# Keys of two heads from one product, and a state-space scan in two strides, in one fused transformer layer

## The chip, the cores and the metric

One Trainium2 chip, one core. The kernel is one launch that computes a whole layer. The metric is the device time of a run in microseconds (us); the kernel before takes 1132.93 us (median of three runs).

## The reference, cut to what matters

The layer mixes tokens in two parallel groups (attention and a state-space layer), projects them back, and then runs a mixture of 32 experts. 1024 latent tokens and 256 context tokens, width 1024, 8 heads.

```python
def mla_project(...):            # per head: 64 key columns without rotation, 32 shared rotary ones
    kv = (rms_norm(ckv, kv_norm_g) @ w_ukv).reshape(*lead, N_HEADS, QK_NOPE_DIM + V_HEAD_DIM)
    k_nope, v = kv[..., :QK_NOPE_DIM], kv[..., QK_NOPE_DIM:]
...
def mla_attend(q_nope, q_rope, k_nope, k_rope, v):
    s = einsum('bqhd,bkhd->bhqk', q_nope, k_nope) + einsum('bqhr,bkr->bhqk', q_rope, k_rope)
    return einsum('bhqk,bkhd->bqhd', softmax(s * SOFTMAX_SCALE), v)
...
def s5_states(u, s0, abar, bbar, reverse):   # x[n] = abar * x[n-1] + (bbar u)[n], complex, per direction
    bu = einsum('bngh,gph->bngp', u, bbar);  bu[:, 0] += abar * s0
    return associative_scan(combine, (abar, bu), axis=1)
```

The context tokens are scanned first from a zero state; the latent scan starts from the context's last state.

## The kernel before, in words

**Order.** All engines run instruction lists written out by hand; the order of the calls in the code is the order on each engine, and loads issued on SP's queue start in that order too. Waits between engines follow from which instruction last wrote or read the same addresses.

**Memory.** `Mem` (line 50) hands out one large SBUF arena in slots of 1024 f32 for each partition (some fifty). `alloc` (line 59) takes a wanted slot (`at`) or else, for sizes of whole slots, the aligned place whose contents were freed longest ago in the order of the code (`c[np.argmin(w[c])]`); a place that was freed most recently comes last. `free` only notes the order. Whoever writes a place next waits on the chip until its last reader is done.

**The scan.** Tokens are grouped in chunks of 8, so that there are 32 context and 128 latent chunks. `chunk_input(g)` (line 796) computes, for each of 32 groups, what a chunk adds to the state, into `Wc` (32 chunks) and `Wl` (128 chunks), with 2 x 32 f32 for each chunk and partition (real and imaginary parts, 32 groups; both directions and 64 states lie on the partitions). Lines 1194 to 1199 then run the recurrence over chunks on GpSimd (POOL), one chunk after the other: a product of the last state with `a8` (the eighth power of abar as a 2 x 2 form, 128 elements for each partition) into `sw`, and two additions of 64 elements. `xc` keeps the state after the context.

```python
    for n in range(1, 160):
        tt(sw.f, Wn(n - 1)[:, None].to_broadcast([128, 2, 2, G]), a8.f, OP.mult, Gp)
        tt(Wn(n), Wn(n), sw.f[:, 0], OP.add, Gp)
        tt(Wn(n), Wn(n), sw.f[:, 1, ::-1], OP.add, Gp)
```

**Attention.** The loop at line 1200 runs over heads h = -1 to 7, and for each over ten key tiles kt of 128 keys. In h = -1 it computes the `values` of each tile, the row maxima (`peak`) of head 0, and one step of `ada()` for each kt; in the other rounds `scores` of the head, `gain` (weights times values), the maxima of the next head and the queries of the head after it. Products in f32 precision are three matmuls of rounded halves (`mm3`, lines 258 to 260). `keys(nxt)` and `keys_c(nxt)` at kt = 0 of round h compute head h+1's 64 key rows for the latent and the context keys and split them into a rounded part `kh` (ScalarE, ACT) and a rest `kl` (VectorE, DVE). Three pairs of PSUM banks go round (`ring2`).

**ada.** `ada()` (line 1012) multiplies the modulation vectors with 16 blocks of 1 MB (`in_wada`), loaded on SP (line 1018) into a buffer of two slots each, one step for each kt of h = -1 and of h = 0, to kt = 6; the block loaded in step n is used by the matmuls of line 1022 in step n+1. In the kernel before the first four blocks lie from slots 12, 20, 24 and 26, and the next ones in the same four places in turn, to the end of h = -1.

**Before the loop.** Lines 1174 to 1190 compute head 0's keys and queries among the last chunk inputs. `shared(i)` (line 845) copies the rotary key rows from `kr` (slots 6.88 to 8.12), the second time just ahead of the scan, and then `kr` and `U` (slots 24 to 29, the chunk inputs' moving operand) are freed.

**Who reads the scan.** `readout()` (line 1031) is stepped from round h = 6 on: at kt = 1 its first loads, at kt = 3 `state(0)`, which copies `Wl` on DVE (line 1053) and ACT.

Of the kernel before, what the change touches and what calls it, by code (L numbers as in the profile page):

```python
# [16 lines left out]
OP = mybir.AluOpType  # L17
# [4 lines left out]
NT = 1024  # L22
NC = 256
H = 8
NOPE, ROPE, VD = 64, 32, 64
G, P, HG = 32, 64, 16
# [197 lines left out]
def body(ctx, tc, a, out):  # L224
    nc = tc.nc
    V, A, Gp, PE, SP = nc.vector, nc.scalar, nc.gpsimd, nc.tensor, nc.sync
# [7 lines left out]
    ps = pp.tile([128, 8, 512], F32, name="ps")  # L234

    def buf(*shape, name="", at=None, zone=None):
        return Buf(nc, zone or mem, shape, name, at)
# [9 lines left out]
    def cp(o, i, scale=1.0):  # L247
        A.activation(o, i, AF.Copy, scale=scale)  # L248

    def tt(o, x, y, op, e=None):  # L250
        (e or V).tensor_tensor(o, x, y, op=op)  # L251

    def split(lo_r, raw, hi_r, hi_f):
        cp(hi_r, raw)
        tt(lo_r, raw, hi_f, OP.subtract)

    def mm3(o, lh, ll, rh, rl, start, stop_):
        PE.matmul(o, lh, rh, start=start, stop=False)  # L258
        PE.matmul(o, lh, rl, start=False, stop=False)  # L259
        PE.matmul(o, ll, rh, start=False, stop=stop_)  # L260
# [25 lines left out]
    a8 = buf(2, 2, G, name="a8", at=-1)  # L286
# [7 lines left out]
    sw, xc = buf(2, 2, G, name="scan", at=-1), buf(2, G, name="xc", at=-1)  # L294
# [447 lines left out]
    for i in range(3):  # L742
# [3 lines left out]
        for ft in (2, 3):  # L746
            b = rA()
# [31 lines left out]
    Wl = buf(128, 2, G, name="Wl", at=-1)  # L779
    Wc = buf(32, 2, G, name="Wc", at=-1)  # L780
# [12 lines left out]
    def Wn(n):  # L793
        return Wc.f[:, n] if n < 32 else Wl.f[:, n - 32]

    def chunk_input(g):
        wi, gl, b = wis[g // 8], g % 8, rS()
        for ri in range(2):
            o = slice(ri * 160, ri * 160 + 160)
            PE.matmul(ps[0:64, b, o], wi.f[:, gl, ri, 0:64], U.f[:, g, 0:160], start=True, stop=True)  # L800
            PE.matmul(ps[64:128, b, o], wi.f[:, gl, ri, 64:128], U.f[:, g, 32:192][:, ::-1],
                      start=True, stop=True)
        src = ps[:, b, 0:320].rearrange("p (r n) -> p r n", r=2)
        for w_, c0, n in ((Wc, 0, 32), (Wl, 32, 128)):
            dst = w_.f[:, :, :, g].rearrange("p n r -> p r n")
            if g % 2:
                cp(dst, src[:, :, c0:c0 + n])
            else:
                V.tensor_copy(dst, src[:, :, c0:c0 + n])  # L809
        if gl == 7:  # L810
            wi.free()

    rS = Ring([6, 7])
    wkv_l, wkv_h = buf(D, name="wkv_l", at=10), buf(D, name="wkv_h", at=10)
# [18 lines left out]
    ring2 = Ring([(0, 1), (2, 3), (4, 5)])  # L833
    NB = 2
    kh = [buf(NT + NC, name="kh", at=33) for _ in range(NB)]
    kl = [buf(NT + NC, name="kl", at=33) for _ in range(NB)]
    rS.items = [6, 7, 3]
    for g in range(16, 24):
        chunk_input(g)
        side_.tick()  # L840
        if g > 21:
            k = g - 22
            split(wuq_l[k].r, wuq_l[k].f, wuq_h[k].r, wuq_h[k].g)

    def shared(i):

        V.tensor_scalar(kh[i].r[96:97, :], kr.f[64:65], 0.0, 1.0, op0=OP.mult, op1=OP.add)
        cp(kh[i].r[64:96], kr.f[64:96])
        tt(kl[i].r[64:96], kr.f[64:96], kh[i].g[64:96], OP.subtract)
# [5 lines left out]
    def flat(d):  # L855
        return ps[:, d[0]:d[0] + 2, :].rearrange("p a n -> p (a n)")

    def ck(o, n):
        lo, hi = ckn[o // 512]
        return hi.r[:, o % 512:o % 512 + n], lo.r[:, o % 512:o % 512 + n]  # L860
# [6 lines left out]
    def values(kt):  # L867
        mm3(ps[:, 6, :], *ck(kt * 128, 128), wkv_h.r[:, 512:], wkv_l.r[:, 512:], True, True)
        cp(v.f[:, kt], ps[:, 6, :])

    def keys(a_):
        d, i = ring2(), a_.i
        for hf in range(2):
            mm3(ps[0:64, d[hf], :], wkv_h.r[:, a_.hs], wkv_l.r[:, a_.hs], *ck(hf * 512, 512), True, True)
        p = flat(d)[0:64]
        cp(kh[i].r[0:64, 0:NT], p)
        tt(kl[i].r[0:64, 0:NT], p, kh[i].g[0:64, 0:NT], OP.subtract)

    def keys_c(a_):
        b, i = ring2()[0], a_.i  # L880
        p = ps[0:64, b, 0:NC]
        mm3(p, wkv_h.r[:, a_.hs], wkv_l.r[:, a_.hs], *ck(NT, NC), True, True)
        cp(kh[i].r[0:64, NT:], p)
        tt(kl[i].r[0:64, NT:], p, kh[i].g[0:64, NT:], OP.subtract)

    def queries(a_):
        d = a_.d = ring2()
# [23 lines left out]
    def peak(a_, q):  # L911

        if q == 0:
            a_.mx = buf(2, 8, name="mx")
        d = ring2()
        for hf in range(2):
            PE.matmul(ps[:, d[hf], :], a_.qh.r[0:96, q * 128:(q + 1) * 128],  # L917
                      kh[a_.i].r[0:96, hf * 512:hf * 512 + 512], start=True, stop=True)
        V.reduce_max(a_.mx.f[:, 0, q:q + 1], flat(d), axis=AX.X)  # L919
# [22 lines left out]
    def scores(a_, kt):  # L942
        i, xh, x = a_.i, a_.qh, a_.ql
        ks = slice(kt * 128, (kt + 1) * 128)
        d = ring2()
        for hf in range(2):
            o, q_ = ps[:, d[hf], :], slice(hf * 512, hf * 512 + 512)
            PE.matmul(o, kh[i].r[0:97, ks], xh.r[0:97, q_], start=True, stop=False)  # L948
            PE.matmul(o, kh[i].r[0:96, ks], x.r[0:96, q_], start=False, stop=False)
            PE.matmul(o, kl[i].r[0:96, ks], xh.r[0:96, q_], start=False, stop=True)  # L950
        p = a_.p[kt] = buf(NT, name="P")
        A.activation(p.f, flat(d), AF.Exp, scale=SCALE)  # L952

    def gain(a_, kt):

        p = a_.p[kt]
        for hf in range(2):
            PE.matmul(ps[hf * 64:hf * 64 + 64, 6, :], v.f[:, kt, a_.hs], p.f[:, hf * 512:hf * 512 + 512],  # L958
                      start=kt == 0, stop=kt == NK - 1)
        if kt == 1:  # L960
            a_.acc = buf(NT, name="acc")
            tt(a_.acc.f, a_.p[0].f, p.f, OP.add)
            a_.p[0].free()
        elif kt:
            tt(a_.acc.f, a_.acc.f, p.f, OP.add)
        if kt:
            p.free()
        if kt == NK - 1:
            a_.o = buf(512, name="o")
            cp(a_.o.f, ps[:, 6, :])  # L970
            a_.ql.free(), a_.qh.free()
# [200 lines left out]
    TILES = ((), (0,), (1,), (2, 3), (4,), (5,), (6,), (7,), (), ())  # L1172
    heads = [Head(h) for h in range(H)]
    side_.drain()
    shared(0)
    keys(heads[0])
    keys_c(heads[0])
    chunk_input(24)
    chunk_input(25)
    queries(heads[0])  # L1180
# [10 lines left out]
    for w_ in (ccl, sig, shx, scx):  # L1191
        w_.free()
    v = buf(NK, 512, name="v", at=28)
    for n in range(1, 160):
        tt(sw.f, Wn(n - 1)[:, None].to_broadcast([128, 2, 2, G]), a8.f, OP.mult, Gp)
        tt(Wn(n), Wn(n), sw.f[:, 0], OP.add, Gp)
        tt(Wn(n), Wn(n), sw.f[:, 1, ::-1], OP.add, Gp)
        if n == 31:
            Gp.tensor_copy(xc.f, Wn(31))
    for h in range(-1, H):  # L1200
        cur, nxt, nn, prev = (heads[i] if 0 <= i < H else None for i in (h, h + 1, h + 2, h - 1))
        for kt in range(NK):
            if cur and nxt and kt == 0:
                keys(nxt)
                keys_c(nxt)
            if cur:
                scores(cur, kt)
            else:
                values(kt)
                next(aux, None)  # L1210
            if kt:
                if cur:
                    gain(cur, kt - 1)
            elif prev:
                gain(prev, NK - 1)
            if prev and 1 <= kt <= 4:
                (sums, inverse, divide, finish_head)[kt - 1](prev)
            if nxt:
                for q in TILES[kt]:
                    peak(nxt, q)  # L1220
                if kt in (1, 5):
                    peak_c(nxt, kt - 1)
                if kt == 7:
                    peak_all(nxt)
                if kt == 8:
                    peak_row(nxt)
            if nn:
                if kt == 7:
                    queries(nn)
                    turned(nn)  # L1230
                if kt == 8:
                    rotate(nn)
                if kt == 9:
                    parts(nn)
            if h == 0:
                next(aux, None)
            if h == 0 and kt == 5:
                Wc.free()
            if h == H - 2 and kt == 1:
                for w_ in [wkv_l, wkv_h] + wuq_l + wuq_h + [w_ for q in ckn + cqn[0] + cqn[1] for w_ in q]:  # L1240
                    w_.free()
                cs.free(), bada.free()
            if (h - H + 2) * NK + kt == RO or (h - H + 2) * NK + kt >= RO2:
                next(ro, None)
            if (h, kt) == (H - 2, 3) or h == H - 1 and kt:
                next(sd, None)
# [139 lines left out]
    for ft in range(4):  # L1386
        d = rG_()
# [609 lines left out]
    o = ps[:, 7, 0:256].rearrange("p (a n) -> p a n", a=2)  # L1997
# [6 lines left out]
    for s in range(8):  # L2004
        mm(s, 0)
        i = s - 1
# [177 lines left out]
```

## Time and profile before

| | |
|---|---|
| median of three runs | 1132.93 us (1132.74 to 1136.99) |
| profiled execution, own time | 1129.01 us |
| its span, first to last instruction | 1127.2 us |
| busy: TensorE (PE) / DVE / ACT / POOL | 994.9 / 692.2 / 453.7 / 394.6 us |
| mean granted TensorE clock | 0.947 of full speed |

Times in the profile are us from the span's start. L251, L248 and the like are lines of the kernel; since a helper `tt` issues all two-input operations, they all carry L251, and all ACT copies L248. `m_f` and `m_r` are places of the arena, `ps` is PSUM. SPq is SP's queue of loads.

### The profile page before, as it was taken

The numbers are of one execution on the slowest core, as the hardware profiler recorded it, in microseconds if no ns is written. First come the engines' busy times: TensorE is split into PE (matmuls) and PEld (weight loads), VectorE is DVE, ScalarE is ACT, GpSimd is POOL, SyncE is SP. The second block draws the span as 40 slices with busy tenths as digits, with TensorE's granted clock in tenths as the row PEclk, the third lists the DMA queues.
The fourth block names the chain that finished last, engine by engine and source line by source line (L and its number), as shares of the span: only waits on it lengthen the run. The fifth ranks groups of instructions, "written<-read, shape, count | busy, mean of one in ns | idle before, by whom it ended". The sixth has DMA issues, their size and how long they took to land.

```text
span 1127.2 us, 14731 instructions
## 1 busy us (share of the span) xinstructions
PE 994.9 (88%) x5266; PEld 635.6 (56%) x5266; DVE 692.2 (61%) x1059; ACT 453.7 (40%) x618; POOL 394.6 (35%) x588
## 2 busy tenths in 40 slices
PE   5998999799999999989999999939999999778840
PEld 2686776454556555657667778734565556444410
DVE  8796833756778877876276448983782545522317
ACT  4442223542544454447656445312442333421206
POOL 0000000388888888870300105320222232111113
PEclk8998999899999999999999999859999999899885
DMA  9664482464000000138640243498789999999946
GB/s 357 259 214 147 150 279 96 180 268 150 1 1 1 1 1 1 33 104 203 214 132 19 75 177 148 162 343 303 226 276 341 345 363 343 340 355 357 353 130 254
DMA packets 66110, 216.98 MB, mean 192 GB/s; under 512 B 10996, under 2 KB 15732, under 8 KB 63476
## 3 DMA queue, kind: packets, MB, share of 16 engines
q1 hardware_dynamic: 57072, 194.99, 48.2%
q0 software_dynamic: 8816, 20.99, 7.4%
q8 instruction: 42, 0.69, 0.2%
q14 instruction: 32, 0.26, 0.1%
q10 hardware_dynamic: 148, 0.05, 0.0%
HBM read 187.70 MB, written 39.31 MB: 201 GB/s over the span
## 4 chain that ended last, share of the span: by engine, by line
PE 25%; DMA 23%; POOL 23%; DVE 14%; issue 11%; ACT 3%; SPq 1%; DVEq 0%; POOLq 0%; ACTq 0%
POOL m_f L251 22%; DMA Yd<-m_f,m_f 18%; DVE m_f L251 7%; PE ps L258 4%; PE ps L260 4%; PE ps L259 4%; PE ps L1903 3%; DVE m_r L251 2%; DMA m_f<-Rd 2%; PE ps L800 1%; DMA m_f<-in_cT 1%; ACT m_r L248 1%; PE ps L958 1%; PE ps L1954 1%; DVE m_f L1856 1%
## 5 line engine op out<-in xcount | busy, mean ns | idle before, releaser
L251 POOL TENSOR_TENSOR m_f<-m_f,m_f 128x64 f32<-128x64 f32 (+1 forms) x477 | 249.5, 523 | 56.1 <-DVE m_f L809 18.8
L251 DVE TENSOR_TENSOR m_f<-m_f 128x1024 f32<-128x1024 f32 (+10 forms) x186 | 171.9, 935 | 51.4 <-ACT m_f L248 20.9
L248 ACT ACTIVATE m_f<-ps 128x512 f32<-128x512 f32 (+5 forms) x187 | 96.6, 550 | 233.8 <-PE ps L1939 67.7
L251 DVE TENSOR_TENSOR m_r<-m_f,m_r 128x1024 fp32r<-128x1024 f32 (+3 forms) x112 | 129.1, 1163 | 85.2 <-ACT m_r L248 82.7
L248 ACT ACTIVATE m_r<-m_f 128x1024 fp32r<-128x1024 f32 (+4 forms) x113 | 111.7, 996 | 99.1 <-DMA m_f<-in_wx 38.9
L952 ACT ACTIVATE m_f<-ps 128x1024 f32<-128x1024 f32 x80 | 81.8, 1023 | 120.6 <-PE ps L950 119.6
L1966 POOL DMA_INDIRECT Yd<-m_f,m_f x27 | 44.0, 1631 | 239.1 <-DVE m_f L251 179.7
L258 PE MATMUL ps<-m_r 128*128 128x512 f32 (+1 forms) x304 | 124.2, 409 | 2.9 <-ACT m_r L248 2.9
L259 PE MATMUL ps<-m_r 128*128 128x512 f32 (+1 forms) x304 | 117.0, 385 | 0.8 <-DVE m_r L251 0.7
L260 PE MATMUL ps<-m_r 128*128 128x512 f32 (+1 forms) x304 | 116.5, 383 | 0.3 <-DVE m_r L251 0.3
L276 POOL TENSOR_TENSOR m_f<-m_f,m_f 128x1 f32<-128x1 f32 (+3 forms) x23 | 24.6, 1069 | 243.3 <-DVE m_f L596 114.3
L919 DVE TENSOR_REDUCE m_f<-ps 128x1 f32<-128x1024 f32 x64 | 77.5, 1221 | 46.5 <-PE ps L917 46.4
L258 PE MATMUL ps<-m_r,m_r 128*128 128x512 f32 (+2 forms) x202 | 82.7, 409 | 5.7 <-DVE m_f L646 2.1
L251 DVE TENSOR_TENSOR m_f<-m_f,m_f 128x576 f32<-128x576 f32 (+9 forms) x154 | 81.7, 569 | 9.5 <-DMA Rd<-m_f 5.7
L958 PE MATMUL ps<-m_f,m_f 128*64 128x512 f32 x320 | 86.3, 618 | 0.0
L259 PE MATMUL ps<-m_r,m_r 128*128 128x512 f32 (+2 forms) x202 | 80.0, 396 | 0.0
L260 PE MATMUL ps<-m_r,m_r 128*128 128x512 f32 (+2 forms) x202 | 79.9, 396 | 0.0
L251 DVE TENSOR_TENSOR m_f<-ps,m_f 128x512 f32<-128x512 f32 (+3 forms) x68 | 49.2, 735 | 47.9 <-PE ps L1954 20.2
L258 PEld LDWEIGHTS ps<-m_r 128*128 128x128 f32 x304 | 59.4, 195 | 20.1 <-issue 8.3
L948 PE MATMUL ps<-m_r,m_r 97*128 97x512 f32 x160 | 66.9, 418 | 3.8 <-DVE m_r L251 3.8
L1954 PE MATMUL ps<-m_f,m_f 128*128 128x512 f32 x152 | 68.6, 594 | 0.5 <-ACT m_f L248 0.5
L260 PEld LDWEIGHTS ps<-m_r 128*128 128x128 f32 x304 | 59.3, 195 | 11.8 <-DVE m_r L251 0.7
(289 smaller groups left out, 1612.7 us busy)
## 6 DMA issues: line engine op xcount, KB each, us to landing
m_f<-in_wx SPq DMA_DIRECT2D x192, 512.0 KB
m_f<-in_wada SPq DMA_DIRECT2D x24, 1024.0 KB
Rd<-m_f SPq DMA_DIRECT2D x8, 576.0 KB
m_f<-Rd SPq DMA_DIRECT2D x8, 576.0 KB
m_f<-in_win SPq DMA_DIRECT2D x8, 512.0 KB
m_f<-in_xT SPq DMA_DIRECT2D x8, 512.0 KB
Wid<-m_f SPq DMA_DIRECT2D x8, 512.0 KB
m_f<-Wid SPq DMA_DIRECT2D x4, 1024.0 KB
```

The source lines that it names most:

```text
L248: A.activation(o, i, AF.Copy, scale=scale)
L251: (e or V).tensor_tensor(o, x, y, op=op)
L258: PE.matmul(o, lh, rh, start=start, stop=False)
L259: PE.matmul(o, lh, rl, start=False, stop=False)
L260: PE.matmul(o, ll, rh, start=False, stop=stop_)
L919: V.reduce_max(a_.mx.f[:, 0, q:q + 1], flat(d), axis=AX.X)
L948: PE.matmul(o, kh[i].r[0:97, ks], xh.r[0:97, q_], start=True, stop=False)
L952: A.activation(p.f, flat(d), AF.Exp, scale=SCALE)
L958: PE.matmul(ps[hf * 64:hf * 64 + 64, 6, :], v.f[:, kt, a_.hs], p.f[:, hf * 512:hf * 512 + 512], start=kt == 0, stop=kt == NK - 1)
L1903: PE.matmul(o, xh.f[:, c_], wl.f[:, ns], start=start, stop=stop_)
L1954: PE.matmul(ps[:, b, :], it.zt.f[:, k], it.lo[4 + k].f[:, ns], start=k == 0, stop=k == 1)
L1966: Gp.indirect_dma_start(out=Yd, out_offset=bass.IndirectOffsetOnAxis(ap=ix, axis=0), in_=y.f, in_offset=None, bounds_check=NT - 1, oob_is_ ...
```

## The change

Two edits. **Keys:** for an even head, one product with 128 stationary columns gives the keys of this head and the next; the second head's 64 rows are copied by ACT to a new buffer `kp`. For an odd head, `keys_b` splits `kp` into `kh` and `kl` and has no product. **Scan:** with `a16`, the square of `a8`, each odd chunk first takes in the even chunk ahead of it, eight such pairs in one operation (`from_last`, with a scratch buffer `sb`); then the odd chunks alone are run in sequence; then the even ones take in their predecessors, eight at a time. All of it stays on GpSimd. `kp`, `sb` and `a16` are new buffers of the arena; the last two are freed in the code behind the scan, ahead of the loop over heads.

```diff
     def keys(a_):
-        d, i = ring2(), a_.i
-        for hf in range(2):
-            mm3(ps[0:64, d[hf], :], wkv_h.r[:, a_.hs], wkv_l.r[:, a_.hs], *ck(hf * 512, 512), True, True)
-        p = flat(d)[0:64]
-        cp(kh[i].r[0:64, 0:NT], p)
-        tt(kl[i].r[0:64, 0:NT], p, kh[i].g[0:64, 0:NT], OP.subtract)
-
-    def keys_c(a_):
-        b, i = ring2()[0], a_.i
-        p = ps[0:64, b, 0:NC]
-        mm3(p, wkv_h.r[:, a_.hs], wkv_l.r[:, a_.hs], *ck(NT, NC), True, True)
-        cp(kh[i].r[0:64, NT:], p)
-        tt(kl[i].r[0:64, NT:], p, kh[i].g[0:64, NT:], OP.subtract)
+        i, hs = a_.i, slice(a_.h * 64, a_.h * 64 + 128)
+        for o, n in ((0, NT), (NT, NC)):
+            d = ring2()
+            for c_ in range(o, o + n, 512):
+                w_ = min(512, n)
+                mm3(ps[:, d[(c_ - o) // 512], 0:w_], wkv_h.r[:, hs], wkv_l.r[:, hs], *ck(c_, w_), True, True)
+            p, c_ = flat(d)[:, 0:n], slice(o, o + n)
+            cp(kh[i].r[0:64, c_], p[0:64])
+            tt(kl[i].r[0:64, c_], p[0:64], kh[i].g[0:64, c_], OP.subtract)
+            cp(kp.f[0:64, c_], p[64:128])
+
+    def keys_b(a_):
+        split(kl[a_.i].r[0:64], kp.f[0:64], kh[a_.i].r[0:64], kh[a_.i].g[0:64])
+        if a_.h == H - 1:
+            kp.free()
...
+    kp = buf(NT + NC, name="kp", at=8.75)
     shared(0)
     keys(heads[0])
-    keys_c(heads[0])
...
     v = buf(NK, 512, name="v", at=28)
-    for n in range(1, 160):
-        tt(sw.f, Wn(n - 1)[:, None].to_broadcast([128, 2, 2, G]), a8.f, OP.mult, Gp)
-        tt(Wn(n), Wn(n), sw.f[:, 0], OP.add, Gp)
-        tt(Wn(n), Wn(n), sw.f[:, 1, ::-1], OP.add, Gp)
-        if n == 31:
+
+    NSC = 8
+    sb, a16 = buf(2, NSC, 2, G, name="sb", at=26), buf(2, 2, G, name="a16", at=8)
+    for k, (p, q) in enumerate(((0, 0), (0, 1))):
+        tt(a16.f[:, k, 0], a8.f[:, p, 0], a8.f[:, q, 0], OP.mult, Gp)
...
+    def from_last(w, x):
+        m = w.shape[1]
+        for k in range(2):
+            tt(sb.f[:, k, 0:m], x, a8.f[:, k][:, None].to_broadcast([128, m, 2, G]), OP.mult, Gp)
+        tt(w, w, sb.f[:, 0, 0:m], OP.add, Gp)
+        tt(w, w, sb.f[:, 1, 0:m, ::-1], OP.add, Gp)
+
+    for w_, n0, n1 in ((Wc, 0, 32), (Wl, 32, 160)):
+        for n in range(0, n1 - n0, 2 * NSC):
+            from_last(w_.f[:, n + 1:n + 2 * NSC:2], w_.f[:, n:n + 2 * NSC:2])
+        for n in range(max(n0 + 1, 3), n1, 2):
+            tt(sw.f, Wn(n - 2)[:, None].to_broadcast([128, 2, 2, G]), a16.f, OP.mult, Gp)
+            tt(Wn(n), Wn(n), sw.f[:, 0], OP.add, Gp)
+            tt(Wn(n), Wn(n), sw.f[:, 1, ::-1], OP.add, Gp)
+        if not n0:
             Gp.tensor_copy(xc.f, Wn(31))
+    from_last(Wl.f[:, 0:1], xc.f[:, None])
+    for n in range(2, 128, 2 * NSC):
+        m = min(n + 2 * NSC, 128)
+        from_last(Wl.f[:, n:m:2], Wl.f[:, n - 1:m - 1:2])
+    sb.free(), a16.free()
     for h in range(-1, H):
...
             if cur and nxt and kt == 0:
-                keys(nxt)
-                keys_c(nxt)
+                (keys_b if nxt.h % 2 else keys)(nxt)
```

The lines left out make `a16` from `a8`: eight operations of 32 elements, seven of them with two inputs.

## Rows read from the trace of the kernel before

**Rows 1.** The page's busy times of each engine, with share and instructions.
```profile
PE 994.9 (88%) x5266; PEld 635.6 (56%) x5266; DVE 692.2 (61%) x1059; ACT 453.7 (40%) x618; POOL 394.6 (35%) x588
```
**Rows 2.** Windows: stretch, length, busy time of each engine, clock, DMA share, GB/s.
```profile
222.00:240.00 18.00, 18.00 (x99) 9.47 (x99) 12.13 (x11) 3.58 (x6) 14.79 (x42) 0.98 0.96 376
270.00:470.00 200.00, 197.63 (x951) 113.59 (x948) 155.01 (x147) 90.33 (x103) 175.15 (x318) 1.00 0.01 5
```
**Rows 3.** Timeline around `state(0)`: start, length, engine, line, idle time before, its releaser.
```profile
497.93 0.73 PE L917 MATMUL ps<-m_r,m_r 96*128 96x512 f32 x2
500.02 1.01 DVE L1053 COPY m_f<-m_f 64x1016 f32<-64x1016 f32 x1 [4.21 <-POOL m_f L251]
502.88 0.80 PE L1081 MATMUL ps<-m_f,m_f 128*128 128x128 f32 x2 [4.22 <-DVE m_f L1109]
```
**Rows 4.** Chain of waits: the scan's last additions that `state(0)` needs.
```profile
499.67 0.33 POOL m_f L251
```
**Rows 5.** Timeline of POOL: the scan's beginning, merged.
```profile
215.15 46.80 POOL L251 TENSOR_TENSOR m_f<-m_f,m_f 128x128 f32<-128x128 f32 x93 [18.82 <-DVE m_f L809]
```
**Rows 6.** Timeline of SP: loads of `in_wada`, the first, second, fourth and fifth.
```profile
198.02 0.33 SPq L1018 DMA_DIRECT2D m_f<-in_wada  x1
214.10 0.33 SPq L1018 DMA_DIRECT2D m_f<-in_wada  x1
214.96 0.42 SPq L1018 DMA_DIRECT2D m_f<-in_wada  x1
221.25 0.33 SPq L1018 DMA_DIRECT2D m_f<-in_wada  x1
```
**Rows 7.** Waits of SP's queue: total us, times, longest.
```profile
SPq L1039 <- PE ps L260: 201.1, 1, 201.1
...
SPq L1018 <- PE ps L801: 27.1, 2, 15.7
```
**Rows 8.** Timeline of PE in h = -1, kt = 4.
```profile
228.47 0.40 PE L260 MATMUL ps<-m_r,m_r 128*128 128x512 f32 x1
...
228.80 1.06 PE L1022 MATMUL ps<-m_f,m_f 128*32 128x512 f32 x8
```
**Rows 9.** Timeline of the second `shared`, on DVE.
```profile
216.36 1.49 DVE L251 TENSOR_TENSOR m_r<-m_f,m_r 32x1280 fp32r<-32x1280 f32 x1
```
**Rows 10.** POOL's groups by shape, 222 to 240 us: count, busy us, mean ns, idle.
```profile
L251 POOL TENSOR_TENSOR m_f<-m_f,m_f 128x64 f32<-128x64 f32 x28 | 9.0, 320 | 2.2
L251 POOL TENSOR_TENSOR m_f<-m_f,m_f 128x128 f32<-128x128 f32 x14 | 6.4, 458 | 1.1
```
**Rows 11.** POOL's groups by shape, 500 to 620 us.
```profile
L251 POOL TENSOR_TENSOR m_f<-m_f 128x1024 f32<-128x1024 f32 x2 | 4.7, 2360 | 6.0 <-DMA m_f<-in_wo 6.0
```
**Rows 12.** POOL's groups by shape, 270 to 470 us.
```profile
L251 POOL TENSOR_TENSOR m_f<-m_f,m_f 128x64 f32<-128x64 f32 x212 | 104.4, 493 | 16.6
L251 POOL TENSOR_TENSOR m_f<-m_f,m_f 128x128 f32<-128x128 f32 x106 | 71.2, 672 | 8.3
```
**Rows 13.** Chain of waits: one of the scan's additions on POOL.
```profile
284.37 1.40 POOL m_f L251
```
**Rows 14.** Timeline of DVE at the same moment.
```profile
284.22 1.22 DVE L251 TENSOR_TENSOR m_f<-m_f 128x1024 f32<-128x1024 f32 x1
```
**Rows 15.** Timeline of `keys`, kt = 0 of round 6.
```profile
476.97 0.45 PE L258 MATMUL ps<-m_r,m_r 128*64 128x512 f32 x1
...
478.75 0.40 PE L948 MATMUL ps<-m_r,m_r 97*128 97x512 f32 x1
...
478.99 1.27 ACT L248 ACTIVATE m_r<-ps 64x1024 fp32r<-64x1024 f32 x2
```
**Rows 16.** Windows: the stretch after PE's short stop at 213 to 215 us.
```profile
215.50:222.80 7.30, 6.58 (x20) 3.16 (x21) 2.74 (x3) 1.82 (x3) 6.28 (x14) 0.53 0.96 400
```

More of the change, by code (lines that the diff above doesn't have):

```diff
@@ L1193, in body @@
     v = buf(NK, 512, name="v", at=28)
-    for n in range(1, 160):
-        tt(sw.f, Wn(n - 1)[:, None].to_broadcast([128, 2, 2, G]), a8.f, OP.mult, Gp)
-        tt(Wn(n), Wn(n), sw.f[:, 0], OP.add, Gp)
-        tt(Wn(n), Wn(n), sw.f[:, 1, ::-1], OP.add, Gp)
-        if n == 31:
-            Gp.tensor_copy(xc.f, Wn(31))
+    NSC = 8
+    sb, a16 = buf(2, NSC, 2, G, name="sb", at=26), buf(2, 2, G, name="a16", at=8)
+    for k, (p, q) in enumerate(((0, 0), (0, 1))):
+        tt(a16.f[:, k, 0], a8.f[:, p, 0], a8.f[:, q, 0], OP.mult, Gp)
+    tt(a16.f[:, 1, 1], a8.f[:, 1, 0], a8.f[:, 1, 0], OP.mult, Gp)
+    tt(a16.f[:, 0, 0], a16.f[:, 0, 0], a16.f[:, 1, 1], OP.subtract, Gp)
+    tt(a16.f[:, 1, 0], a16.f[:, 1, 0], a16.f[:, 1, 0], OP.add, Gp)
+    Gp.tensor_copy(a16.f[:, 0, 1], a16.f[:, 0, 0])
+    tt(a16.f[:, 1, 1], a8.f[:, 0, 0], a8.f[:, 1, 1], OP.mult, Gp)
+    tt(a16.f[:, 1, 1], a16.f[:, 1, 1], a16.f[:, 1, 1], OP.add, Gp)
+    def from_last(w, x):
[12 more added lines that the diff above has]
+        if not n0:
+            Gp.tensor_copy(xc.f, Wn(31))
+    from_last(Wl.f[:, 0:1], xc.f[:, None])
[3 more added lines that the diff above has]
+    sb.free(), a16.free()
     for h in range(-1, H):
```

## The prediction

> **What bounds the kernel now.** I read the page first: PE is busy for 994.9 of 1127.2 us and no other engine comes near [rows 1]. The windows show that this holds for the stretch of the change above all: from 270 to 470 us, inside the attention loop, PE is busy for 197.6 of 200 us at full clock, while POOL, which runs the scan at the same time, is busy for 175 us [rows 2]. So time saved on POOL is worth something only where PE comes to wait for the scan. The timeline shows one such place: PE's last work ends at 498.66 us, DVE and ACT stand in `state(0)` until POOL's addition that ends at 500.00, and PE goes on at 502.88, after 4.2 us of idleness [rows 3, 4]. These 4.2 us are all that a faster scan can give. Time taken off PE inside the loop counts fully, as long as the scan does not hold it up.
>
> Then I asked the opposite: who could come to wait for the scan that doesn't now? That is settled by memory, since a new writer of a place waits for its last reader. So I followed `alloc` by hand through the calls behind the scan, before and after the change.
>
> **The new wait.** In the kernel before, the loads of `in_wada` in h = -1 take slots 12, 20, 24 and 26. The first is issued at 198.02 us; the next waits for the last chunk input to leave its slot and comes at 214.10, the fourth at 214.96, the fifth (slot 12 again, when its matmuls are over) at 221.25 [rows 6]. That such a wait is made, and that it stops SP's whole queue, the waits show: SP spent 27.1 us on L801's matmuls ahead of these loads, and in another place 201.1 us ahead of the first load of the readout, for the last product that read the queries' and keys' weights, whose place that load takes [rows 7].
>
> The change puts `sb` into slot 26 and frees it ahead of the loop, in the code. At the fourth load, slots 12 and 20 have just been freed by the first two blocks, that is, later than `sb`; slots 24 and 25 hold the third. The place freed longest ago is 26, as before. But now its last reader is not a matmul at 214 us: it is the last addition of the whole scan, which reads `sb`. So the fourth load waits on SP for the end of the scan. Behind it on SP stand the other twelve blocks, and much later the readout's loads. PE needs the fourth block at kt = 4: it does this tile's values and then, at 228.80 us in the kernel before, its L1022 matmuls [rows 8]. PE's list is in order, so PE stops there, and ACT and DVE run dry behind it. POOL's scan needs none of them, so there is no deadlock; everything else waits for POOL.
>
> **When the scan ends.** Its start: `a16` lies at slot 8.00, in the end of `kr`, which the second `shared` still reads on DVE until 216.36 + 1.49 = 217.85 us [rows 9]; now POOL starts at 215.15 [rows 5]. `keys` of head 0 gives ACT 1.3 us more work ahead of that; I cost it at nothing, with 1.3 us as the upper bound.
>
> Its length: undisturbed, an operation of 64 elements takes 0.320 us, one of 128 takes 0.458 [rows 10] and one of 1024 takes 2.360 [rows 11], with some 0.07 us between two: in rows 10, 14 steps of three operations take 9.0 + 6.4 + 2.2 + 1.1 = 18.7 us, 1.33 us for each. No row has 512 elements; the line between 128 and 1024 gives 0.458 + 384 x 0.00212 = 1.27, or 1.34 with the gap. The bounds are the bare slope, 1.09, and four operations of 128, 1.83; I take the line, since three sizes lie close to it.
> - `from_last` has four such operations, 5.4 us. Ten blocks ahead of the sequence: 53.7. Behind it, seven and one of seven chunks (448 elements, 4 x 1.21): 42.4.
> - The sequence: 15 steps in the context and 64 in the latent part, 79 x 1.33 = 105.1.
> - `a16` 8 x 0.32 = 2.6, the copy 0.3, the single chunk 4 x 0.4 = 1.6.
>
> Together 205.7 us. The old scan by the same prices is 159 x 1.33 = 211.5: in bare work the change saves 6 us of 211, for it has half the steps but 40% more elements (159 x 256 = 40,704 before, 79 x 256 + 36,000 now).
>
> Is it undisturbed? The old scan took 215 to 500 us because its operations are stretched in the loop, to 0.493 and 0.672 us [rows 12]: an addition at 284.37 took 1.40 us and ended 0.33 us behind a DVE operation with two SBUF inputs that had begun at 284.22 [rows 13, 14]. When PE has stopped, DVE has no such operation left; and from 222 to 240 us, where DVE only takes maxima from PSUM, POOL is undisturbed already [rows 10]. So the scan ends at 217.9 + 205.7 = 423.6 us.
>
> The Trainium skill, "SBUF — State Buffer", section "SBUF: two separate sides", states this as an exclusive lock: whichever starts first of a VectorE operation with two SBUF inputs and a GpSimd operation has the shared ports to its end. Rows 13 and 14 agree (1.40 us instead of 0.32). By the rule the stopped loop gives 205.7 us; by the mean stretch of rows 12 it would be some 280.
>
> **The sum.** The fourth load then lands: 1 MB at the 376 GB/s of [rows 2] is 2.8 us at least; the fourth load before had landed 13.8 us after its issue at the latest [rows 6, 8]. I take 5, nearer the lower end, because it is now the first in the queue. PE goes on at 428.9 instead of 228.8: +200.1 us. After that the loop runs as before, with these differences:
> - The 4.2 us at `state(0)` are gone, the scan being long over [rows 3].
> - Odd heads 1, 3, 5 and 7 have no product: 478.75 - 476.97 = 1.78 us of PE for each [rows 15], 7.1 together. 128 stationary columns cost an even head no more than 64 did: the time is that of the moving columns.
> - Even heads 2, 4 and 6 give ACT another pair of copies, 1.27 us [rows 15], ahead of the exponentials for which PE waits for a PSUM pair: between 0 and 3.8 us, I take 2. The odd heads' split has the same lengths as before, on the same engines.
> - After its short stop at 213 to 215 us PE had a granted clock of 0.53, mostly the 1.2 GHz level, for 7.3 us [rows 16], which cost 7.3 x 0.47 = 3.4 us. After a stop of 200 us I expect the same again, +3.4; none to twice that.
>
> 200.1 - 4.2 - 7.1 + 2 + 3.4 = +194. The profiled execution's 1129.0 us become 1323; the median of the runs is 3.9 us above that execution, so I forecast 1327 us.
>
> **The rivals.**
> - *No wait.* The fourth load does not wait for `sb`, by another place or another end of it. Then the scan is stretched as before: the old one lost 285 - 210 us, so 205.7 x 285 / 210 = 279, from 217.9 to 497: 3 us earlier than now, and PE, which comes 5 us earlier to `state(0)`, waits 6 us there. The time is about 1130, at best 1124, where all of 4.2 and 7.1 less 2 are saved. This is the case on the other side; it decides if the load lands before 228.8. Against it: the slots follow from the code and the queue does stop for such places [rows 7]. Chance 6%.
> - *Wait and stretch.* POOL's stretch is its own, not DVE's: the scan takes 279 us with nothing beside it, and the time is 1327 + 73 = 1400. Against it: [rows 10], undisturbed beside a busy PE. Chance 2%.
> - *Dear blocks.* An operation over eight separate chunks costs as eight of 64 elements, 8 x 0.32 = 2.56 us: 72 x 1.29 = 93 us more, 1420. Against it: 128 elements in two runs cost 0.458, not 0.64 [rows 10]. Chance 3%.
>
> **How the numbers follow.** The forecast has 89%. Its own range: the slope alone for the blocks (-13 us), a landing in 2.8 (-2), no clock loss (-3), no ACT cost (-2): with most of these 1305. Upwards, blocks half way to 1.83 (+20), a later landing, 1.8 us of ACT and another 3 of clock: 1352. The cases left out have 11%, and some of the forecast's own lies outside, so 8 in 10 is held. A measurement of this kernel can't tell less than 0.5%, 5.7 us, from no change. *No wait* gives 2% to faster and 4% to the same; slower has 94%.
>
> **What would show it.** Right: a gap in PE, DVE and ACT from about 229 to 429 us with POOL at work alone; the fourth load issued at the scan's end and twelve blocks behind it; POOL's 512 element operations at 1.27 us and its steps at 1.33; nothing waiting at `state(0)`; four `keys` less 1.78 us of PE. Wrong: `in_wada` loads going on at 215 to 270 us; or the gap there and its length far from 200 us, which would be the price of the blocks.

## The result, and the profile after

The changed kernel takes 1324.66 us (median of four runs, 1323.08 to 1328.18); the kernel before takes 1132.84 us beside it. The ratio is 1.169 (1.167 to 1.172): 17% slower, as forecast (1327, range 1305 to 1352). The profiled execution took 1323.08 us with a span of 1321.3, which is 194.1 us longer than that of before; the sum of the prediction had +194.

The page of the changed kernel: busy times, and three rows of its 40 slices (33 us each).
```profile
span 1321.3 us, 14507 instructions
...
PE 990.7 (75%) x5230; PEld 631.9 (48%) x5230; DVE 688.5 (52%) x1055; ACT 458.0 (35%) x622; POOL 321.9 (24%) x432
...
PE   6989997000002999999999899998499999987860
...
POOL 0000003898895000000000200144212223211113
PEclk8999998555555999999999999999699999988885
```
Only ACT has more work than in [rows 1], by 4.3 us; PE is busy 4.2 us less, DVE 3.7 and POOL 72.7. What is new is the hole in PE's row, five slices of 0 with a part of one at each end, exactly where POOL is full, and the granted clock at half.

Windows of the changed kernel: stretch, length, busy time of PE, PEld, DVE, ACT, POOL, then clock, DMA share, GB/s.
```profile
222.00:232.00 10.00, 7.42 (x37) 3.99 (x37) 5.94 (x5) 1.79 (x3) 9.61 (x11) 0.96 0.00 0
232.00:420.00 188.00, 0.00 (x0) 0.00 (x0) 0.00 (x0) 0.00 (x0) 164.14 (x303) 0.50 0.02 6
420.00:436.00 16.00, 15.28 (x78) 7.70 (x79) 7.42 (x7) 2.39 (x4) 0.00 (x0) 0.87 0.93 390
```
For 188 us nothing at all runs on PE, DVE and ACT, and next to nothing moves on the DMA engines (6 GB/s), while POOL is at work. At 222 us, where the kernel before moved 376 GB/s [rows 2], the transfers have stopped already: this is a queue that stands, not one that is slow.

Who waits, for whom: the waits of SP's queue.
```profile
SPq L1042 <- PE ps L260: 205.7, 1, 205.7
SPq L1021 <- POOL m_f L251: 200.2, 1, 200.2
```
The waits of PE, 215 to 425 us.
```profile
PE ps L1025 <- DMA m_f<-in_wada: 191.3, 1, 191.3
```
The chain of waits from 414 us: start, length, engine and line.
```profile
414.59 1.14 POOL m_f L251
415.74 4.84 DMA m_f<-in_wada
420.72 1.94 PE ps L1025 x8
```
The timeline of SP: the loads on either side of the hole. The first row is the second and third load in one (x2), the other the fourth with the three behind it (x4).
```profile
214.69 0.81 SPq L1021 DMA_DIRECT2D m_f<-in_wada  x2
...
415.74 2.06 SPq L1021 DMA_DIRECT2D m_f<-in_wada  x4
```
These rows, read from the bottom, are the mechanism. The fourth load of `in_wada`, which before was issued at 214.96 us [rows 6], stands on SP for 200.2 us until POOL's last addition ends, and starts 0.01 us later; 4.84 us on, it has landed, and PE's L1025 (L1022 before) begins at 420.72 instead of 228.80 us [rows 8]. The wait of L1042 in the same view is that of [rows 7], where it is 201.1 us, and holds nothing up.

POOL's groups by shape, 217 to 425 us: count, busy us, mean ns, idle.
```profile
L251 POOL TENSOR_TENSOR m_f<-m_f,m_f 128x512 f32<-128x512 f32 x68 | 83.9, 1263 | 1.3
L251 POOL TENSOR_TENSOR m_f<-m_f,m_f 128x64 f32<-128x64 f32 x162 | 51.3, 318 | 12.5
L251 POOL TENSOR_TENSOR m_f<-m_f,m_f 128x128 f32<-128x128 f32 x79 | 35.8, 453 | 6.0
L251 POOL TENSOR_TENSOR m_f<-m_f,m_f 128x448 f32<-128x448 f32 x4 | 4.4, 1126 | 0.1
```
An operation of 512 elements over eight separate chunks takes 1.263 us, where the line through [rows 10, 11] gave 1.27, but they follow each other without a gap, one every (83.9 + 1.3) / 68 = 1.25 us, where the forecast had added 0.07 to each.

### The profile page after: what moved, and what is told of

It is laid out like the page before. It is cut to its first block, busy times and chain, and to the rows that moved or that the text cites. A ratio compares the mean times of both kernels' runs of the same rounds, so it can differ in the third digit from the quotient of the medians.

```text
span 1321.3 us, 14507 instructions
## 1 busy us (share of the span) xinstructions
PE 990.7 (75%) x5230; PEld 631.9 (48%) x5230; DVE 688.5 (52%) x1055; ACT 458.0 (35%) x622; POOL 321.9 (24%) x432
## 4 chain that ended last, share of the span: by engine, by line
PE 38%; DMA 20%; DVE 14%; POOL 14%; issue 9%; ACT 5%; SPq 0%; DVEq 0%; POOLq 0%; ACTq 0%
DMA Yd<-m_f,m_f 16%; POOL m_f L251 14%; DVE m_f L251 7%; PE ps L961 5%; PE ps L258 4%; PE ps L259 4%; PE ps L260 4%; DVE m_r L251 3%; PE ps L920 3%; PE ps L1933 2%; PE ps L951 2%; PE ps L952 2%; PE ps L953 2%; DMA m_f<-Rd 2%; ACT m_r L248 2%
## 5 line engine op out<-in xcount | busy, mean ns | idle before, releaser
L248 ACT ACTIVATE m_f<-ps 128x512 f32<-128x512 f32 (+5 forms) x195 | 102.1, 557 | 436.0 <-PE ps L260 231.5
L251 DVE TENSOR_TENSOR m_f<-m_f 128x1024 f32<-128x1024 f32 (+10 forms) x186 | 168.6, 917 | 53.5 <-ACT m_f L248 21.0
L251 POOL TENSOR_TENSOR m_f<-m_f,m_f 128x64 f32<-128x64 f32 (+3 forms) x313 | 175.2, 567 | 19.9
L251 DVE TENSOR_TENSOR m_r<-m_f,m_r 128x1024 fp32r<-128x1024 f32 (+4 forms) x116 | 133.7, 1164 | 82.7 <-ACT m_r L248 67.7
L1025 PE MATMUL ps<-m_f,m_f 128*32 128x512 f32 x128 | 18.8, 661 | 191.3 <-DMA m_f<-in_wada 191.3
L248 ACT ACTIVATE m_r<-m_f 128x1024 fp32r<-128x1024 f32 (+5 forms) x117 | 116.3, 1005 | 97.6 <-DMA m_f<-in_wx 37.4
L258 PE MATMUL ps<-m_r 128*128 128x512 f32 (+1 forms) x304 | 122.9, 404 | 2.9 <-ACT m_r L248 2.9
L259 PE MATMUL ps<-m_r 128*128 128x512 f32 (+1 forms) x304 | 115.8, 381 | 0.8 <-DVE m_r L251 0.7
L260 PE MATMUL ps<-m_r 128*128 128x512 f32 (+1 forms) x304 | 115.3, 379 | 0.3 <-DVE m_r L251 0.3
L1025 PEld LDWEIGHTS ps<-m_f,m_f 128*32 128x32 f32 x128 | 2.6, 112 | 197.0 <-issue 196.7
L258 PE MATMUL ps<-m_r,m_r 128*128 128x512 f32 (+1 forms) x190 | 80.3, 423 | 4.3 <-DVE m_f L646 2.2
L260 PE MATMUL ps<-m_r,m_r 128*128 128x512 f32 (+1 forms) x190 | 76.9, 405 | 0.0
L259 PE MATMUL ps<-m_r,m_r 128*128 128x512 f32 (+1 forms) x190 | 76.9, 405 | 0.0
```

## The experiments

Ratios are to the kernel before, run on the same chip beside each, with 95% intervals. A *round* is one head's pass through the loop; "late by" is the start of the row of products of a head's maxima (L937, L940 in the changed kernel), which each round has once, against the same row of before.

**Is it that place, and is it nothing else?** The first pair was made to settle it from both sides. `e1_sb_held` is the changed kernel with the free of the scratch moved behind all the loads:

```diff
-    sb.free(), a16.free()
     for h in range(-1, H):
...
+            if (h, kt) == (H - 1, 0):
+                sb.free(), a16.free()
```


> The changed kernel with one difference: sb and a16 stay taken until the last round of the loop (h = 7, kt = 0), so no load is given slot 26 while the scan runs. Theory (the whole loss is the fourth in_wada load's wait for sb): the 191 us gap in PE is gone and the time is 1122 to 1134 us; the scan, again beside a busy DVE, takes some 279 us and ends near 497, so that it is worth next to nothing. Rival (the two-stride scan or the shared keys are slow by themselves): the time stays above 1200.

`e2_old_scan_slot26` has nothing of the change: the old scan, one chunk after the other, whose scratch is merely put where `sb` lies, and freed ahead of the loop.

```diff
+    sb = buf(8, 2, 2, G, name="sb", at=26)
     for n in range(1, 160):
-        tt(sw.f, Wn(n - 1)[:, None].to_broadcast([128, 2, 2, G]), a8.f, OP.mult, Gp)
-        tt(Wn(n), Wn(n), sw.f[:, 0], OP.add, Gp)
-        tt(Wn(n), Wn(n), sw.f[:, 1, ::-1], OP.add, Gp)
+        tt(sb.f[:, 0], Wn(n - 1)[:, None].to_broadcast([128, 2, 2, G]), a8.f, OP.mult, Gp)
+        tt(Wn(n), Wn(n), sb.f[:, 0, 0], OP.add, Gp)
+        tt(Wn(n), Wn(n), sb.f[:, 0, 1, ::-1], OP.add, Gp)
...
+    sb.free()
```


> The kernel before, scan and keys unchanged, but the scan's scratch is a buffer in slot 26 that is freed in the code ahead of the loop. Theory: the same wait is there without any of the change; POOL runs undisturbed, 159 steps of 1.33 us, so the scan ends near 215 + 212 = 427 us, PE goes on near 432 instead of 229, and the time is 1129 + 203 - 4 + 3 = 1331 us by the profiled execution (1325 to 1340). Rival (the loss belongs to the new scan or the keys): the time stays at 1133.

Measured: e1 1158.95 us, ratio 1.023 (1.020 to 1.026); e2 1329.01 us, ratio 1.175 (1.172 to 1.178). The waits of SP's queue in e2:
```profile
SPq L1018 <- POOL m_f L251: 212.3, 1, 212.3
```
and its chain of waits from 414 us:
```profile
426.48 5.02 DMA m_f<-in_wada
431.63 1.94 PE ps L1022 x8
```
So one re-used place, without two strides and without the new keys, makes a loss as large; and with the place held, 166 of the 192 us are gone. The old scan, beside stopped engines, ran from 214.43 to 426.45 us, 212.0 us long: the 211.5 that the prediction worked out for it. That the two-stride scan is 197.2 us long in the same silence is all that it saves in bare work: 15 us, where the prediction had 6.

But e1 is not the 1122 to 1134 that the mechanism alone would leave. Its windows show PE full at 222 to 240 us:
```profile
222.00:240.00 18.00, 18.00 (x97) 8.52 (x89) 10.74 (x9) 3.59 (x6) 16.43 (x27) 0.89 0.87 318
```
and its timeline of ACT shows a new stop:
```profile
302.74 1.02 ACT L955 ACTIVATE m_f<-ps 128x1024 f32<-128x1024 f32 x1 [18.06 <-POOL m_f L251]
```
An exponential waits 18 us for POOL. To tell which part brings what, the two edits were run apart.

**The two edits apart.** `e3_keys_alone` is the kernel before with the keys' part of the diff; `e4_scan_alone_held` has the scan's part, with the scratch held as in e1.

> The kernel before with the keys edit alone. Theory from the trace after (rounds that make an even head's keys got 2.0 to 3.5 us longer, those with an odd head's 1.5 us shorter, since ACT's extra pair of copies stands ahead of the exponentials): the edit saves nothing in the loop, PE comes to the readout about when it did, and the time is 1130 to 1138 us. Rival (the 7.1 us less of PE count fully, up to the scan's end): PE waits 9 to 11 us at the readout instead of 4.2 and the time is 1130 to 1134; with it the rounds of even heads are as long as before.

> The kernel before with the scan edit alone, sb and a16 held to h = 7. Theory: beside the busy DVE the scan takes 205.7 x 285/210 = 279 us (with 1.24 us for an operation of 512 elements rather 270), ends at 488 to 497 instead of 500, and the 4.2 us at the readout go: 1126 to 1131 us. Rival (longer GpSimd operations hold DVE's two-input operations back, up to 1.3 us each, and PE with them): DVE's 128x1024 additions grow well beyond their mean of 1.275 us, PE falls below 98% busy in the loop, and the time is 1135 to 1150.

Measured: e3 1134.25 us, ratio 1.002 (1.0005 to 1.004); e4 1142.92 us, ratio 1.009 (1.007 to 1.012). In e4's timeline of ACT the stop of e1 is there again, in a copy:
```profile
299.99 1.05 ACT L248 ACTIVATE m_f<-m_f 32x1024 f32<-32x1024 f32 x1 [12.41 <-POOL m_f L251]
```
and its waits of PE, 270 to 320 us, hand it on:
```profile
PE ps L948 <- ACT m_f L952: 11.3, 1, 11.3
```
From that row on e4 is 14.2 us late. It is the same trap a second time. `Wc` (the context's chunks) is freed in the code at h = 0, kt = 5, which in the kernel before came after its last reader, step 32 of the scan. In two strides the first step of the latent part (n = 33) reads chunk 31 from `Wc`, and in POOL's order it stands behind all eight blocks of the latent part. The place of `Wc` goes to new tiles, whose writers now wait for that step.

`e5_scan_held_xc` takes the reader away: `xc` holds the same numbers.

```diff
-            tt(sw.f, Wn(n - 2)[:, None].to_broadcast([128, 2, 2, G]), a16.f, OP.mult, Gp)
+            tt(sw.f, (xc.f if n == 33 else Wn(n - 2))[:, None].to_broadcast([128, 2, 2, G]), a16.f, OP.mult, Gp)
```


> Scan edit alone with sb held (1142.9 us), and the first latent step of the sequence (n = 33) reads the context's last state from its copy xc instead of from Wc; the same values. Theory: Wc's slots 39 and 40 are given to the attention at the end of round 0, and in the two-stride scan step 33 is Wc's last reader, behind the eight latent blocks at 300 us; with xc the last reader is at 253 us, ACT's wait of 12.4 us and PE's of 11.3 us go, and the time is 1129 to 1135 us. Rival (the 10 us of loss come from GpSimd's long operations holding DVE back): the time stays at 1139 to 1143.

`e6_both_held_xc` is e1 with that line.

> The changed kernel with sb held (1159.0 us), and the same reading of xc at n = 33. Theory: ACT's 18.1 us wait for POOL at 302.7 us and the 11.3 us that PE loses with it go: 1139 to 1148 us, and what is left over the scan edit alone is the keys' price beside a DVE that POOL slows. Rival (keys and scan don't meet but in that wait): 1131 to 1135, the sum of the two edits alone.

Measured: e5 1133.15 us, ratio 1.001 (0.998 to 1.003); e6 1140.79 us, ratio 1.007 (1.005 to 1.010). e5 is 9.8 us below e4, and 5.2 us late at the row at which e4 was 14.2; e6 is 18.2 below e1. So e4's time, which lies in the range of its rival, was mostly that of the wait. The scan with two strides, free of both waits, brings no gain. Its last addition ends at 484.5 us (before, the one that `state(0)` needs ends at 500.0 [rows 4]), nobody waits for it at `state(0)`, and the round with `state(0)` catches up 6.1 us. But PE had lost 4.1 us in round 1 and 4.0 in round 5, which are those in which POOL runs the blocks. The groups of DVE, 230 to 470 us, in the kernel before and in e5:
```profile
L251 DVE TENSOR_TENSOR m_f<-m_f 128x1024 f32<-128x1024 f32 x51 | 64.8, 1271 | 0.2
...
L251 DVE TENSOR_TENSOR m_f<-m_f 128x1024 f32<-128x1024 f32 x48 | 68.3, 1423 | 0.2
```
and e5's timeline, one of PE's waits in a block stage, in 12.9 us on POOL without a pause:
```profile
286.49 12.89 POOL L251 TENSOR_TENSOR m_f<-m_f,m_f 128x512 f32<-128x512 f32 x6
291.24 2.20 DVE L251 TENSOR_TENSOR m_f<-m_f 128x1024 f32<-128x1024 f32 x1
293.37 2.29 DVE L251 TENSOR_TENSOR m_r<-m_f,m_r 96x1024 fp32r<-96x1024 f32 x1
295.58 1.54 DVE L251 TENSOR_TENSOR m_r<-ps,m_r 64x1024 fp32r<-64x1024 f32 x2
...
296.84 0.50 PE L948 MATMUL ps<-m_r,m_r 97*128 97x512 f32 x1 [2.97 <-DVE m_r L251]
```
An operation of DVE with two SBUF inputs that takes 1.22 us in [rows 14] takes 2.20 here and the next one 2.29. PE needs what the subtractions behind them on DVE write, from 295.58 on, and stands still for 2.97. Over the whole stretch the mean is 1.423 us, where it was 1.271. The six operations of POOL beside them take 2.1 us each instead of 1.26. The Trainium skill's rule of an exclusive lock ("SBUF — State Buffer", "SBUF: two separate sides") fits this: by it an operation of DVE can lose as much as the whole length of one of POOL. It lost 0.98 us here, and a block's operation takes 1.263 us undisturbed, 2.8 times a step's product (0.453).

`e7_blocks_of_4` halves the length of the blocks' operations (256 elements) and so doubles their number.

```diff
-    NSC = 8
+    NSC = 4
```


> As the scan alone with sb held and xc, with blocks of four pairs (NSC = 4): operations of 256 elements, twice as many. By the line through POOL's sizes an operation takes 0.73 us instead of 1.26, so the bare scan is some 14 us longer and ends near 490, still ahead of the readout. Theory (a longer GpSimd operation keeps DVE's two-input operations waiting for longer): DVE's 128x1024 additions fall from a mean of 1.39 us towards 1.28 and the time is 0 to 4 us below blocks of eight. Rival (DVE's waiting has no price, PE being the bound): the same time within 2 us, or longer if the scan's end comes to the readout.

Measured: 1136.62 us, ratio 1.003 (1.001 to 1.005). The groups of DVE, 230 to 470 us:
```profile
L251 DVE TENSOR_TENSOR m_f<-m_f 128x1024 f32<-128x1024 f32 x50 | 67.0, 1339 | 0.2
```
DVE's operations come down from 1.423 to 1.339 us and the two block stages cost PE 1.3 and 2.8 us instead of 4.1 and 4.0. So what DVE loses goes with the length of POOL's operations, as the theory had it. But the scan then ends at 503.9 us instead of near 490, and DVE in `state(0)` waits for it again (2.71 us): the time is 3.5 us above e5's, not below it. What is saved at one end is paid at the other.

**Why the keys bring nothing.** In e3 the odd heads win 0.5 to 1.0 us each, but each of the even heads 2, 4 and 6 loses 2.2, 3.6 and 3.8. The timeline of the changed kernel shows an even head's keys (round 1, kt = 0), ACT and DVE together:
```profile
485.00 1.00 ACT L248 ACTIVATE m_r<-ps 64x1024 fp32r<-64x1024 f32 x1
486.31 1.21 DVE L251 TENSOR_TENSOR m_r<-ps,m_r 64x1024 fp32r<-64x1024 f32 x1
487.55 1.02 ACT L248 ACTIVATE m_f<-ps 64x1024 f32<-64x1024 f32 x1 [1.55 <-DVE m_r L251]
...
489.86 1.02 ACT L955 ACTIVATE m_f<-ps 128x1024 f32<-128x1024 f32 x1
```
The copy into `kp` does not read what DVE writes, and DVE's operand is another half of the partitions; yet it waits for DVE's subtraction, which reads the same PSUM banks and stands ahead of it in the code. The exponential, for which PE waits, starts 4.86 us after the first copy; before, with one pair of copies, 1.4 (478.99 [rows 15] to 480.40). Two experiments move the copy. `e8_both_held_xc_late_copy` puts it off, in e6, until the gain matmuls of kt = 0 have been issued; `e9_keys_kp_first` is e3 with the copy ahead of the subtraction.

```diff
             cp(kh[i].r[0:64, c_], p[0:64])
+            cp(kp.f[0:64, c_], p[64:128])
             tt(kl[i].r[0:64, c_], p[0:64], kh[i].g[0:64, c_], OP.subtract)
-            cp(kp.f[0:64, c_], p[64:128])
```


> As both edits with sb held and xc, with the copies to kp put behind the exponentials of tile 0 and the copy of the last head's output on ACT, instead of ahead of them. Theory (the even heads' rounds are long because these copies stand ahead of what PE waits for): rounds of even heads get 1 to 2 us shorter each and the time is 3 to 6 us below the run without it. Rival (what PE waits for is the PSUM pair that the copies themselves free): no difference within 2 us, or longer.

> Keys edit alone (1134.3 us), with ACT's copy to kp ahead of DVE's subtraction instead of behind it. Theory (ACT waits 1.5 us for DVE's subtraction, since both read the same PSUM banks, and the next tile's exponentials stand behind that): the rounds of even heads, 2.2 to 3.8 us longer than before in the keys edit alone, get 1 to 2 us shorter each; the scan's end at 500 us still holds the readout, so the time stays at 1131 to 1135. Rival (the price is the copies' own 1.3 us on ACT): the even rounds stay 2 to 4 us longer than before.

Measured: e8 1136.34 us, ratio 1.001 (0.999 to 1.003); e9 1130.85 us, ratio 0.997 (0.995 to 0.999). In e9's timeline of ACT the copies stand back to back, and the exponential comes 2.9 us after the first:
```profile
440.20 1.01 ACT L248 ACTIVATE m_r<-ps 64x1024 fp32r<-64x1024 f32 x1
441.23 1.02 ACT L248 ACTIVATE m_f<-ps 64x1024 f32<-64x1024 f32 x1
...
443.07 1.02 ACT L955 ACTIVATE m_f<-ps 128x1024 f32<-128x1024 f32 x1
```
The even heads now lose 0.5 us each instead of 2.2 to 3.8, the odd ones win 0.5 to 1.0 as in e3. That settles the term for e3. It does not settle e8. Its time is 4.5 us below e6's, as forecast (3 to 6), but not in the way forecast: the rounds of heads 2, 4 and 6 lose 6.0, 1.4 and 9.9 us where those of e6 lose 5.9, 6.5 and 6.9, so one got shorter and one longer, and why stays open. Nor is shown whether the chip itself would make the copy wait; the wait is one that the program carries.

**Are the 4.2 us at `state(0)` to be had?** e9 reaches `state(0)` earlier and waits there, its waits of PE from 480 to 520 us say:
```profile
PE ps L1084 <- DVE m_f L1112: 5.6, 1, 5.6
```
`e10_readout_late` is the kernel before with `state(0)` one key tile later and a step made good at kt = 5; `e11_kp_first_readout_late` is e9 with the same two lines.

```diff
-RO, RO2 = 1, 3
+RO, RO2 = 1, 4
...
+            if (h, kt) == (H - 2, 5):
+                next(ro, None)
```


> The kernel before with the readout's state(0) one tile later (kt = 4 of round 6) and two of its steps at kt = 5. Theory (a faster scan could give the 4.2 us of PE's wait at state(0) and no more): the wait is gone and the time is 3 to 4 us shorter, 1128 to 1130. Rival (the readout's loads, some 10 us each, set its pace afterwards): 1131 to 1134.

> Both of these: keys edit with kp first, old scan, state(0) one tile later. If the keys then cost nothing net, the time is that of the late readout, 1127 to 1131; if even rounds still cost more than the odd ones save, 1131 to 1135.

Measured: e10 1135.27 us, ratio 1.002 (1.000 to 1.004); e11 1133.20 us, ratio 0.999 (0.997 to 1.001). e10 lies above both of its ranges, e11 in the upper of its two. The waits of PE in e10, 488 to 600 us:
```profile
PE ps L1081 <- DMA m_f<-Ud: 3.1, 2, 2.2
PE ps L1082 <- DMA m_f<-Rd: 3.1, 3, 1.6
PE ps L1081 <- ACT m_f L952: 3.0, 1, 3.0
```
Two of them are for the readout's own loads, and the third is still the wait for the scan. DVE in `state(0)` waited 2.15 us for POOL, to 501.3, and ACT's part as long as that; the exponential that PE waits for stands behind it in ACT's timeline:
```profile
501.32 1.92 ACT L248 ACTIVATE m_f<-m_f 64x1016 f32<-64x1016 f32 x1 [2.69 <-POOL m_f L251]
...
503.26 1.02 ACT L952 ACTIVATE m_f<-ps 128x1024 f32<-128x1024 f32 x1
```
So e10 did not take the wait away, and says nothing of what it is worth. The runs in which the scan ends long before do: from the row of scores ahead of `state(0)` to the next one behind it, PE takes 12.0 us in the kernel before (495.0 to 507.0) and 6.1 in the changed kernel (692.6 to 698.7), in e2 and in e5. That is 5.9 us and not 4.2, because the kernel before comes back from its wait at the lower clock level; its windows:
```profile
502.80:506.90 4.10, 4.02 (x23) 4.02 (x24) 4.05 (x7) 3.49 (x4) 1.07 (x2) 0.62 0.70 219
```

**All three causes mended.** `e12_both_held_xc_kp_first` is the whole change with the scratch held, `xc` at n = 33 and the copy first.

> The changed kernel mended in three places: sb held, xc read at n = 33, kp copied ahead of the subtraction (without the last: 1140.8 us). Theory (the same wait of ACT for DVE, dearer here since DVE is itself held up by POOL's long operations): 3 to 6 us less, 1134 to 1138, still no faster than the kernel before, because the block operations cost DVE and PE some 8 us where the readout's wait gives back 4.2. Rival (that wait is no more than its 1.5 us): 1138 to 1141.

Measured: 1132.71 us, ratio 0.999 (0.997 to 1.001): 8.1 us below e6, more than the 3 to 6 forecast, and why the copy is worth more here than in e3 is not shown. From the changed kernel to here the steps are 1324.7, 1159.0 with the scratch held, 1140.8 with `xc`, 1132.7 with the copy first. Both edits, free of their waits, come out even with the kernel before. Of the versions tried, only e9, the keys alone with the copy first, has an interval wholly below 1, by 0.1% to 0.5%; that is no more than the 0.5% which the prediction counts as no change.

## Why the prediction was right, and where its sum was not

**The wait** was right in each of its steps: the place that the fourth load takes, its last reader, the queue that stops, the tile at which PE stops. e1 and e2 show that it is the cause, and that it needs nothing else of the change.

**The total** was right partly by luck: terms that were wrong by up to 9 us cancel. The table compares the two profiled executions (+194.1 us). The one of before lies 3.8 us under the median of its runs and that of the changed kernel 1.6 under; by the medians the difference is 191.8. Line by line, in us:

| term | forecast | measured |
|---|---|---|
| scan starts / ends | 217.9 / 423.6 | 218.50 / 415.73 |
| fourth block lands after | 5 | 4.84 |
| PE goes on, against before | +200.1 | +191.9 |
| from there to the maxima of head 0 (the clock) | +3.4 | +1.6 |
| keys of heads 1 to 6 | -3.3 | +5.6 |
| keys of head 7, and `state(0)` | -6.0 | -8.95 |
| the readout and all behind it | 0 | +3.9 |
| sum | +194.2 | +194.1 |

The maxima rows in the changed kernel are these, eight for each head: duration, first and last start (before, 242.4 and 530.2 us, so +193.5 and +190.2).
```profile
L940 PE MATMUL ps<-m_r,m_r x64: 219/222/227, 435.9 to 720.4; 128*1 128x128 f32 x64
```
- *A slip of addition:* 423.6 + 5 is 428.6 and not the "428.9" of the prediction, so that PE's +200.1 should read +199.8; the total stays at +194.
- *The scan's length* was over-estimated by 8.5 us (197.2 for 205.7): the blocks took 83.9 + 1.3 + 4.4 + 0.1 = 89.7 us by the groups above instead of 96.1, since the gap of 0.07 us that I added to each operation isn't there; `a16`, to the first block at 220.31, took 1.8 instead of 2.6; and what is left for the sequence, the copy and the single chunk is 105.7 instead of 107.0.
- *The keys* are the term that was mis-sized: "-7.1" for the odd heads and "+2" for ACT's copies. Heads 1 to 6 come out at +5.6. The odd heads 3 and 5 win 1.5 us each, near the 1.78 forecast (0.3 of it is the scan's absence: in e2, with the old keys and no scan beside them, rounds 1 to 5 are 0.24 to 0.31 us shorter too), but heads 2, 4 and 6 lose 2.0, 3.5 and 2.0, not 2 among them. The step that failed is "give ACT another pair of copies", 1.27 us: I counted the copies' own time and not that, in the order of the code, one of them stands behind a DVE operation on the same banks. e3 against e9 shows it.
- *The 4.2 us at `state(0)`* were under-priced. The -8.95 are 1.5 for head 7's keys, 5.9 across `state(0)` as shown above, and 1.5 behind it, where the kernel before waits 1.3 us for a load of `Rd`. "These 4.2 us are all that a faster scan can give" leaves out the clock after the wait, which the prediction priced for the long stop and not for this one.
- *The readout and all behind it* stood at nothing. Between two rows of scores of the last round (540.3 to 554.2 us before, 730.6 to 748.8 now) 4.3 us are lost. The waits of PE from 705 to 800 us, all but 0.2 us of these two in that stretch:
```profile
PE ps L1085 <- DMA m_f<-Rd: 2.8, 3, 1.3
PE ps L1084 <- DMA m_f<-Ud: 1.4, 1, 1.4
```
  In the like stretch the kernel before waits 1.4 us for `Rd` and not for `Ud`. This is not the price of the wait that went: e3 and e9, in which PE still waits at `state(0)`, lose 4.0 us in the same place, and e2 and e5, in which it doesn't, 0.9 and 0.3. It comes with the new keys, and in e10 without them (4.0); why, stays open.
- *The clock*: 1.6 us of loss instead of 3.4.

**The rivals.** *Wait and stretch* and *dear blocks* are excluded: the operations of the silent stretch took 0.318, 0.453 and 1.263 us. *No wait* was priced at about 1130; had it come, the time would have been 1159 (e1). Its stretched scan was forecast to last 279 us and lasts 266 in e5 and 262 in e4, so the scan's end is not what made it wrong; what it lacked was the second re-used place, `Wc`, and the price of the long operations to DVE. I followed `alloc` for the places that the change frees, and not for the places whose *readers* it moves.

## What to carry to other kernels

A free in the code says nothing of when the last reader is done: where a slow engine runs far behind the code, as a scan on POOL does, look for every buffer that it reads late, the new scratch and the old ones whose readers were put in another order, and ask who gets their places and which queue that writer stands in. An engine with spare time is not free of cost to its neighbours: making its operations fewer and longer can stretch those of an engine that the bound one waits for. And a short wait of the bound engine costs more than its length when the engine comes back from it at the lower clock; to learn what it is worth, take the wait away, and look in the trace whether it is gone.

## What the runs showed of the hardware beside that

- After its stop of 190 us PE came back at the lower clock level, but only for 4 us; the windows of the changed kernel:
```profile
420.60:424.60 4.00, 3.88 (x13) 1.68 (x13) 0.75 (x1) 0.00 (x0) 0.00 (x0) 0.55 1.02 430
424.60:436.00 11.40, 11.40 (x66) 6.02 (x66) 6.67 (x7) 2.39 (x4) 0.00 (x0) 1.00 0.90 374
```
  In the kernel before it had a clock of 0.53 for 7.3 us after the short stop at 213 to 215 us [rows 16], and of 0.62 for 4.1 us after the 4.2 us at `state(0)`. The stop of 190 us cost 1.6 us, the two short ones 3.4 and 1.7.
- On POOL operations of 512 elements follow each other without a gap, while the shorter ones have some 0.08 us ahead of each (12.5 us over 162 and 6.0 over 79 in the groups above).
- The load that PE waited for took 4.84 and 5.02 us from issue to landing for 1 MB, with the loads issued behind it under way at the same time.
